# Row sums of the modulation traced in smaller portions, and eight weight casts moved from ACT to GpSimd, in a two-layer diffusion step

## The chip, the cores and the metric

The kernel runs on one core of a Trainium2 chip. The metric is the device time of one execution in microseconds. Times of a profile are counted from the start of its span.

## The reference

One inference step of a two-layer trunk over 128 context tokens and 512 latent tokens of 1024 features (640 tokens in five tiles of 128). Layer 0 is gated grouped-query attention, layer 1 a gated linear recurrence. Cut to what matters here:

```python
mod = silu(cond) @ ada_w[i] + ada_b[i]          # per layer: shift, scale, gate; cond is c (latent) or c_ctx (context)
sh, sc, g = split(mod, 3)
h = x * (1 + sc) + sh
# layer 0
q, k, v, gate = split(h @ w_in)                 # 16 query heads, 4 key heads of 64; gate of width 1024
q, k = rms_norm(q), rms_norm(k)                 # latent tokens also rotary
o = softmax(q k^T / 8) v                        # latent: over cache, context and latent keys
out = (o * silu(gate)) @ w_out
x = layer_norm(alpha * x + g * out)
# layer 1: the same around a gated recurrence (HGRN2, both directions)
```

## The kernel before

Matrix products run in a reduced-width 32-bit format and are kept accurate by splitting: each operand is a high part (a cast of the value) and a low part (the value minus its high part), and a product is three matmuls, high by high, high by low and low by high. Weights come from memory in pieces of 128 x 1024 into a ring of three raw buffers (`rawp`). `split_piece` (L232) takes the next raw piece, makes the high part on ACT (L240) and the low part on DVE or GpSimd (L241); `pump` issues the next loads on the SP queue in the fixed order of `order`.

The attention input weights are cut into chunks of 256 columns: 0 to 3 are queries (one chunk serves one key head), 6 to 9 the gate. The first half of the program, up to the end of attention, is traced in the order of the code and then ordered by a scheduler that plays a time line: on each engine it issues what is ready, and among ready instructions the one traced first. `keep_in_program_order` (`pin`) ties an instruction behind the one traced before it on its engine; all loads of this half on SP are tied so. `tc.issue_after(ins)` ties the instructions traced inside it to come after `ins`, if they are on the engine of `ins`. Buffers of a ring are handed out in traced order.

Stages of the first half:

- Lead-in, keys and values: the modulated input `hhi`/`hlo`, the key and value projection.
- `lead_in`, gate projection: query chunk 0 (`pmm`), then 16 half tiles (`gps`, L349 to L351, 24 matmuls each) of gate chunks 6 to 9, each ended by a SiLU on ACT (L854) into `gs`. The jobs in `later` (three query jobs `q_job`, four key splits) are taken one at every second step, and `settle` traces their transposes (`qps`, L702) one such step after. A query job on DVE is: scale by the norm (`qn`, L615), rotate (L654 to L658), cast the high part on ACT (L693), subtract on DVE (L694). The half tiles, the queries and the transposes share six PSUM places; three of them (`bank1`) hold the queries of chunk 0 until their jobs read them.
- Modulation of layer 1, shift and scale: 16 jobs (`COLS`), each a raw block of 128 x 1024 loaded on SP, and two row sums on DVE (`ada_cols`, L335: block times SiLU of the conditioning, summed along the row, for latent and context). Twelve jobs run in `lead_in` with blocks in a ring of two (`adar`, loads at L840); their product is spilled into the part of `gs` that is filled last. Four late jobs run in `cols_gen` within chunk 1 and take their blocks from the raw ring; they spill into the ring `s2` (two buffers, which the query and key splits use too).
- Attention over chunks 0 to 3 (`att_gen`), woven with a side stream: query chunks 1 to 3 (`q_gen`: weights, projection `qmm`, norm, split, transposes), each with a `fill` generator (chunk 1: the late jobs; chunks 2 and 3: the gate row of the modulation, `ada_gen`, matmuls at L284 with blocks `ada_s`), then `prefetch_gen`, which splits four pieces of the output weights (`wo_gen`), and the split of `gs`. A score tile (`sc`, L869 and L870) goes through a maximum on DVE (L964), an exponential on ACT (L969), a scaling on GpSimd (L975), transposes (L982), copies (L874) and the product with the values (L896). GpSimd also raises to the power -1/2 for the norms (L191).

The second half, the output projection and the recurrence, is issued in the order of the code.

Of the kernel before, what the change touches and what calls it, by code (L numbers as in the profile page):

```python
# [11 lines left out]
F32 = mybir.dt.float32  # L12
F32R = mybir.dt.float32r
U8 = mybir.dt.uint8
AF = mybir.ActivationFunctionType
ALU = mybir.AluOpType
AX = mybir.AxisListType

P = 128
D = 1024  # L20
KT = D // P
# [106 lines left out]
def drain(gen):  # L128
    for _ in gen:
        pass  # L130
# [3 lines left out]
def hybrid_step(ctx: ExitStack, tc: tile.TileContext, a: dict, o: dict):  # L134
    nc = tc.nc
    PSUM = bass.MemoryType.PSUM

    def pool(name, bufs, **kw):
        return tc.tile_pool(name=name, bufs=bufs, **kw)
# [15 lines left out]
    class Phase:  # L155
        def __init__(self, n2, n1):
            self.st = ExitStack()
            if n2:
                pools["b2"] = self.st.enter_context(pool("b2", n2, space=PSUM))
            pools.pop("b1", None)  # L160
            if n1:
                pools["b1"] = self.st.enter_context(pool("b1", n1, space=PSUM))
# [22 lines left out]
    shsc = [const.tile([P, 2, KT, 2], F32, name=f"shsc{i}") for i in range(2)]  # L185
# [43 lines left out]
            return a[name][c, i]  # L229
        return a[name][c][:, i * 1024:(i + 1) * 1024]  # L230

    def split_piece(hi, lo, src, lo_eng=None, after=()):  # L232
        pump()
        got, raw = ahead.popleft()
        assert got == src, (got, src)
        raw = raw[:, :hi.shape[-1]]
        with ExitStack() as st:
            for ins in after:
                st.enter_context(tc.issue_after(ins))
            nc.scalar.copy(hi, raw)  # L240
            (lo_eng or nc.gpsimd).tensor_tensor(lo, raw, hi.bitcast(F32), ALU.subtract)  # L241
        pump()

# [4 lines left out]
    def wtile(shape, dt, tag, name):  # L248
        ring = rings[turn[tag] % len(rings)]
        turn[tag] += 1  # L250
        return ring.tile(shape, dt, tag=tag, name=name)

    class Weights:


        def __init__(self, name, c, engs=None, after=()):
            self.h, self.l = [], []
            for i in range(2):
                hi = wtile([P, 1024], F32R, tag="whi", name="whi")
                lo = wtile([P, 1024], F32R, tag="wlo", name="wlo")  # L260
                split_piece(hi, lo, (name, c, i), engs and engs[i], after)
                self.h.append(hi[:].rearrange("p (k n) -> p k n", k=4))
                self.l.append(lo[:].rearrange("p (k n) -> p k n", k=4))

# [6 lines left out]
    def take(src):  # L271
        pump()
        got, raw = ahead.popleft()
        assert got == src, (got, src)
        return raw
# [52 lines left out]
            gate[0] = gsp.tile([P, 2, D], F32, tag="gate", name="gate0")  # L328
            gate_load(0, nc.gpsimd)

    def ada_cols(job, raw, spill):

        s, ft = job
        for c in range(2):
            nc.vector.scalar_tensor_tensor(spill, raw, 1.0, silb[:, c, :], ALU.mult, ALU.mult,  # L335
                                           accum_out=shsc[1][:, s, ft, c:c + 1])
        if ft == KT - 1:
            nc.vector.tensor_tensor(shsc[1][:, s], shsc[1][:, s], view(adab, (3 + s) * KT, [[1, KT], [0, 2]]), ALU.add)

    def cols_gen():  # L340
        for job in COLS[len(COLS) - COLS_LATE:]:
            ada_cols(job, take(("ada_c",) + job), prep.tile([P, D], F32, tag="s2", name="spill", bufs=2))
            pump()
            yield

    def feat_mms(ps, w, mt, j, hhi, hlo):
        c, t = slice(mt * P, (mt + 1) * P), slice(*HALVES[j])
# [5 lines left out]
    last_qmm = []  # L353
# [22 lines left out]
    PIECES = [(nh, i) for nh in range(2) for i in range(4)]  # L376
# [44 lines left out]
    silb = gsp.tile([P, 2, D], F32, tag="gate", name="silb")  # L421
# [7 lines left out]
    prep = pq.enter_context(pool("prep", 1))  # L429
# [155 lines left out]
    gs = gsp.tile([P, KT, NT], F32, tag="gs", name="gs")  # L585
# [101 lines left out]
    last_split = []  # L687
# [24 lines left out]

    def q_gen(c, X, fill):

        w = Weights("attn_w_in", c, (nc.vector, nc.vector), tuple(last_split))
        yield
        if c > 1:
            next(fill)
            yield
        pend = None  # L720
        for tt0, n in UNITS:
            ps = yield from tok_unit(w, tt0, n, "qmm")
            rstd = rms_stat(ps, n)
            r = rope_raw(ps, tt0, n, cosq, sinq, qg)
            yield
            if pend:
                for i in range(pend[1]):
                    pend[0](i)
                    yield
            next(fill, None)  # L730
            yield
            yield
            qn = rms_scale(r, n, rstd)
            yield
            pend = (q_split(qn, tt0, n, c % 2, X, bank1), n)
        yield
        for _ in fill:
            yield
        for i in range(pend[1]):
            pend[0](i)  # L740
            yield
# [11 lines left out]
    def lead_in(att):  # L753
# [59 lines left out]
        w = ws.pop(0)  # L813
        q0, kr = [], {}
        for n, (tt0, m) in enumerate(UNITS):
            ps = bank_any("pmm")
# [18 lines left out]
        raws = deque()  # L835

        def cols_load():
            if cols:
                raw = adar.tile([P, D], F32, tag="raw", name="adaraw")
                pin(nc.sync.dma_start(raw, piece(("ada_c",) + cols[0])))  # L840
                raws.append((cols.popleft(), raw))

        for _ in range(2):
            cols_load()
        step = 0
        for ch in range(6, 10):
            if ch < 9:
                ws[ch + 1] = Weights("attn_w_in", ch + 1, LEAD_LO)
            w = ws.pop(ch)
            for mt in range(2):  # L850
                for j, (t0, t1) in enumerate(HALVES):
                    ps = bank_any("gps")
                    feat_mms(ps, w, mt, j, hhi, hlo)
                    nc.scalar.activation(gs[:, 2 * (ch - 6) + mt, t0:t1], ps[:, :320], AF.Silu)  # L854
                    step += 1
                    if step % 2 or not later:
                        settle()
                    if step % 2 and later:
                        later.pop(0)()
                    if raws:  # L860
                        ada_cols(*raws.popleft(), gs[:, KT - 2:, :].rearrange("p a b -> p (a b)")[:, :D])
                        cols_load()
                    if step > 16 - EARLY:
                        next(att)
        assert not raws


    def score_mms(out, X, c, h, t0, k0, k1):
# [225 lines left out]

    wo = {}

    def wo_gen(layer, pieces, wpool):
        for nh, i in pieces:
            hi = wpool.tile([P, 1024], F32R, tag=f"wohi{nh}{i}", name="wohi")
            lo = wpool.tile([P, 1024], F32R, tag=f"wolo{nh}{i}", name="wolo")  # L1100
            wo[nh, i] = tuple(t[:].rearrange("p (k n) -> p k n", k=2) for t in (hi, lo))
            split_piece(hi, lo, ("attn_w_out" if layer == 0 else "rec_w_out", nh, i), nc.vector)
            yield

    def split_act(dst_hi, dst_lo, src, eng=None):
# [9 lines left out]
    woa = []  # L1115

    def prefetch_gen():
        wb.close()
        pq.close()
        woa.append(ws.enter_context(pool("woa", 1)))  # L1120
        yield from wo_gen(0, PIECES[:4], woa[0])

    def q_next(c):
        Xs[c] = xq[c % 2].tile([P, 4, NT], F32R, tag="X", name=f"X{c}")
# [651 lines left out]
```

## Time and profile before

| | |
|---|---|
| three runs | 846.48, 842.91, 846.51 us; median 846.48 |
| profiled execution | 844.78 us, span 843.0 us, granted TensorE clock 0.99 |
| TensorE (PE) busy | 808.0 us, 96% of the span |
| DVE busy | 559.9 us, 66% |
| ACT busy | 386.5 us, 46% |
| GpSimd (POOL) busy | 215.8 us, 26% |
| row sums in the lead-in | 24, the first at 71.6 us, the last at 122.0 us |
| row sums in chunk 1 | 8, from 144.3 to 185.5 us |

A row of the order of time gives the start, the length, the engine, the line, the operation, what it writes and reads, its size, and in brackets how long the engine was idle before it and for whom it waited. Rows of the same kind that follow each other are merged (x8). A row of the windows gives, for a stretch, its length, the busy time of PE, PEld, DVE, ACT and POOL with the number of instructions, the granted clock, the share of the DMA engines and GB/s. A row of the groups gives the count, the busy time, the mean in ns and the idle time of the engine before them with its causes.

### The profile page before, as it was taken

The page shows a single profiled execution, that of the slowest core. Times are in us where ns is not written, and L with a number is a line of the kernel's source. Part 1 is how long each engine was busy: PE and PEld are TensorE (multiplying, and loading weights), DVE is VectorE, ACT ScalarE, POOL GpSimd, SP SyncE. Part 2 cuts the span into 40 slices and gives each one's busy share as a digit, 9 for nine tenths or more (in the row PEclk, how much of TensorE's full clock was granted, in tenths as well). Part 3 has the DMA queues.
Part 4 walks back from the last instruction along what each step waited for, and adds up shares of the span by engine and source line. Part 5 has one row for each costly group of instructions (what it writes and reads, how often), then busy time and mean ns, then how long its engine had stood idle before and what let it go on. Part 6 is the DMA issues. An engine that isn't in the chain of part 4 may idle for free.

```text
span 843.0 us, 19206 instructions
## 1 busy us (share of the span) xinstructions
PE 808.0 (96%) x8025; PEld 729.2 (87%) x8025; DVE 559.9 (66%) x996; ACT 386.5 (46%) x782; POOL 215.8 (26%) x261
## 2 busy tenths in 40 slices
PE   8999899989999988999999999999999999999994
PEld 6789799878878766888999999999999999998774
DVE  4568882795657674776438575767668575858477
ACT  2252354674656776222434444435434544445232
POOL 0123001443344833010001304143333314121121
PEclk9999899999999999999999999999999999999998
DMA  9944451114151230630322322231322312324041
GB/s 325 397 145 165 151 175 52 51 54 148 51 200 51 101 100 1 225 125 35 108 69 68 103 72 82 83 109 51 107 89 83 99 61 89 120 65 157 23 161 75
DMA packets 34326, 93.28 MB, mean 111 GB/s; under 512 B 5040, under 2 KB 12224, under 8 KB 34240
## 3 DMA queue, kind: packets, MB, share of 16 engines
q1 hardware_dynamic: 23568, 74.10, 25.9%
q0 software_dynamic: 4768, 14.18, 5.4%
q10 hardware_dynamic: 5904, 3.78, 1.5%
q8 instruction: 63, 1.03, 0.5%
q14 instruction: 23, 0.19, 0.1%
HBM read 82.85 MB, written 9.19 MB: 109 GB/s over the span
## 4 chain that ended last, share of the span: by engine, by line
PE 82%; DVE 9%; ACT 2%; DMA 2%; issue 2%; POOL 1%; SPq 0%; DVEq 0%; ACTq 0%; POOLq 0%
PE rps L1319 7%; PE rps L1320 7%; PE rps L1321 7%; PE vgps L1309 5%; PE vgps L1311 5%; PE vgps L1310 5%; PE pot L896 4%; PE outp L1158 4%; PE outp L1160 3%; PE outp L1159 3%; PE pt L982 3%; PE lv L1452 2%; PE acc L536 2%; PE gps L349 2%; PE sc L869 2%
## 5 line engine op out<-in xcount | busy, mean ns | idle before, releaser
L1319 PE MATMUL rps<-h1hi,rhi 128*128 128x320 f32 x368 | 118.4, 322 | 0.0
L1320 PE MATMUL rps<-h1lo,rhi 128*128 128x320 f32 x368 | 113.9, 309 | 0.0
L1321 PE MATMUL rps<-h1hi,rlo 128*128 128x320 f32 x368 | 113.8, 309 | 0.0
L975 POOL TENSOR_SCALAR p<-p,rc 128x640 f32<-128x640 f32 x64 | 58.8, 921 | 116.6 <-DVE rc L974 102.3
L1319 PEld LDWEIGHTS rps<-h1hi,rhi 128*128 128x128 f32 x368 | 69.2, 188 | 1.3
L1320 PEld LDWEIGHTS rps<-h1lo,rhi 128*128 128x128 f32 x368 | 69.3, 188 | 0.0
L1321 PEld LDWEIGHTS rps<-h1hi,rlo 128*128 128x128 f32 x368 | 69.1, 188 | 0.0
L241 DVE TENSOR_TENSOR rlo<-raw,rhi 128x1024 fp32r<-128x1024 f32 x32 | 45.0, 1409 | 33.8 <-ACT rhi L240 33.8
L964 DVE TENSOR_REDUCE nm<-sc 128x1 f32<-128x640 f32 x64 | 52.0, 818 | 23.2 <-PE sc L870 22.8
L1480 POOL COPY At<-near 32x160 f32<-32x160 f32 x32 | 14.0, 438 | 196.8 <-DVE near L1442 195.8
L969 ACT ACTIVATE p<-sc,nm 128x640 f32<-128x640 f32 x64 | 51.2, 802 | 27.2 <-DVE nm L964 19.3
L240 ACT CAST rhi<-raw 128x1024 fp32r<-128x1024 f32 x32 | 33.6, 1049 | 52.0 <-PE rps L1320 48.8
L1430 ACT COPY kc<-A 128x640 f32<-128x640 f32 x40 | 32.2, 806 | 54.4 <-DVE A L1461 50.5
L1309 PE MATMUL vgps<-rhi,h1hi 128*128 128x256 f32 x180 | 51.5, 286 | 0.0
L1310 PE MATMUL vgps<-rlo,h1hi 128*128 128x256 f32 x180 | 50.9, 283 | 0.0
L1311 PE MATMUL vgps<-rhi,h1lo 128*128 128x256 f32 x180 | 50.9, 283 | 0.0
L982 PE MATMUL pt<-small,p 128*128 128x128 f32 x320 | 48.6, 276 | 1.4 <-ACT pts L874 0.9
L869 PE MATMUL sc<-kk,X 128*128 128x320 f32 x128 | 42.6, 343 | 6.1 <-ACT p L969 6.0
L874 ACT COPY pts<-pt 128x512 f32<-128x512 f32 x64 | 35.8, 591 | 24.4 <-PE pt L982 24.1
L982 PEld LDWEIGHTS pt<-small,p 128*128 128x128 f32 x320 | 37.1, 140 | 7.8 <-issue 5.3
L1309 PE MATMUL vgps<-wspare,h1hi 128*128 128x256 f32 x140 | 41.8, 298 | 0.0
L896 PE MATMUL pot<-pts,vv 128*64 128x256 f32 x320 | 38.9, 386 | 2.4 <-DVE pts L874 2.4
(301 smaller groups left out, 2423.6 us busy)
## 6 DMA issues: line engine op xcount, KB each, us to landing
raw<-in_rec_w_in SPq DMA_DIRECT2D x40, 512.0 KB, 3.7
raw<-in_ada_m SPq DMA_DIRECT2D x16, 512.0 KB, 8.0
raw<-in_attn_w_in SPq DMA_DIRECT2D x16, 512.0 KB, 4.2
raw<-in_ada_s SPq DMA_DIRECT2D x16, 512.0 KB, 4.4
adaraw<-in_ada_c SPq DMA_DIRECT2D x12, 512.0 KB, 3.8
raw<-in_attn_w_out SPq DMA_DIRECT2D x8, 512.0 KB, 4.1
raw<-in_rec_w_out SPq DMA_DIRECT2D x8, 512.0 KB, 3.5
x1d<-y SPq DMA_DIRECT2D x5, 512.0 KB, 2.6
```

The lines of the kernel that those rows point to most:

```text
L869: nc.tensor.matmul(out, X[:, h, t0:t0 + P], kk[:, c, k0:k1], start=True, stop=False)
L896: nc.tensor.matmul(pot[j * HD:(j + 1) * HD, :CW], vv[:, slot, c * HD:(c + 1) * HD], moving[j], start=first, stop=last)
L964: nc.vector.tensor_reduce(nm[:, 0:1], sc[:, :, :320], AX.XY, ALU.max, negate=True)
L969: return nc.scalar.activation(halves(p[:]), sc[:, :, :320], AF.Exp, bias=nm[:, 0:1], accum_out=su[:, 0:1])
L975: nc.gpsimd.tensor_scalar(p, p, rs[:, 0:1], 1.0, ALU.mult, ALU.mult)
L982: nc.tensor.transpose(pt[:, i * 256 + q * P:i * 256 + (q + 1) * P], ps[q][:, (k0 + i) * P:(k0 + i + 1) * P], ident)
L1309: nc.tensor.matmul(out, h1hi[:, k, t], hi, start=(k == 0), stop=False)
L1310: nc.tensor.matmul(out, h1hi[:, k, t], lo, start=False, stop=False)
L1311: nc.tensor.matmul(out, h1lo[:, k, t], hi, start=False, stop=(k == KT - 1))
L1319: nc.tensor.matmul(ps[:, j, :320], hi[:, k, :], h1hi[:, k, t], start=(k == 0), stop=False)
L1320: nc.tensor.matmul(ps[:, j, :320], hi[:, k, :], h1lo[:, k, t], start=False, stop=False)
L1321: nc.tensor.matmul(ps[:, j, :320], lo[:, k, :], h1hi[:, k, t], start=False, stop=(k == KT - 1))
```

## The change

- `ada_cols` becomes a generator: after each of its two row sums it yields, and each sum is traced inside `tc.issue_after` of an instruction that its caller names: the newest SiLU of the gate projection in `lead_in`, the newest query matmul in `cols_gen`.
- In `lead_in` a step advances this generator once in steps 1 to 6 and twice from step 7 on; before, each step ran one whole job. The next block is loaded when a job has ended, as before. Sums traced after the twelfth SiLU spill into the ring `s2`.
- In `cols_gen` each `next` of the fill now runs one sum, not a job.
- The high-part casts of query chunks 2 and 3 (four) and of the first four pieces of the attention output weights (four) are issued on GpSimd.

```diff
-    def split_piece(hi, lo, src, lo_eng=None, after=()):
+    def split_piece(hi, lo, src, lo_eng=None, after=(), hi_copy=None):
...
-            nc.scalar.copy(hi, raw)
+            (hi_copy or nc.scalar.copy)(hi, raw)
             (lo_eng or nc.gpsimd).tensor_tensor(lo, raw, hi.bitcast(F32), ALU.subtract)
...
-    def ada_cols(job, raw, spill):
+    def ada_cols(job, raw, spill, after):
 
         s, ft = job
         for c in range(2):
-            nc.vector.scalar_tensor_tensor(spill, raw, 1.0, silb[:, c, :], ALU.mult, ALU.mult,
-                                           accum_out=shsc[1][:, s, ft, c:c + 1])
+            with tc.issue_after(after()):
+                nc.vector.scalar_tensor_tensor(spill(), raw, 1.0, silb[:, c, :], ALU.mult, ALU.mult,
+                                               accum_out=shsc[1][:, s, ft, c:c + 1])
+            yield
...
+    def spare():
+        return prep.tile([P, D], F32, tag="s2", name="spill", bufs=2)
+
     def cols_gen():
         for job in COLS[len(COLS) - COLS_LATE:]:
-            ada_cols(job, take(("ada_c",) + job), prep.tile([P, D], F32, tag="s2", name="spill", bufs=2))
+            yield from ada_cols(job, take(("ada_c",) + job), spare, lambda: last_qmm[0])
             pump()
-            yield
...
-        w = Weights("attn_w_in", c, (nc.vector, nc.vector), tuple(last_split))
+        w = Weights("attn_w_in", c, (nc.vector, nc.vector), tuple(last_split),
+                    nc.gpsimd.tensor_copy if c > 1 else None)
...
+        silus = []
+
+        def spill():
+            return gs[:, KT - 2:, :].rearrange("p a b -> p (a b)")[:, :D] if len(silus) <= 12 else spare()
+
+        def cols_steps():
+            while raws:
+                yield from ada_cols(*raws.popleft(), spill, lambda: silus[-1])
+                cols_load()
+
+        cgen = cols_steps()
...
-                    nc.scalar.activation(gs[:, 2 * (ch - 6) + mt, t0:t1], ps[:, :320], AF.Silu)
+                    silus.append(nc.scalar.activation(gs[:, 2 * (ch - 6) + mt, t0:t1], ps[:, :320], AF.Silu).ins)
...
-                    if raws:
-                        ada_cols(*raws.popleft(), gs[:, KT - 2:, :].rearrange("p a b -> p (a b)")[:, :D])
-                        cols_load()
+                    for _ in range(1 if step < 7 else 2):
+                        next(cgen, None)
...
-    def wo_gen(layer, pieces, wpool):
+    def wo_gen(layer, pieces, wpool, hi_copy=None):
...
-            split_piece(hi, lo, ("attn_w_out" if layer == 0 else "rec_w_out", nh, i), nc.vector)
+            split_piece(hi, lo, ("attn_w_out" if layer == 0 else "rec_w_out", nh, i), nc.vector, (), hi_copy)
...
-        yield from wo_gen(0, PIECES[:4], woa[0])
+        yield from wo_gen(0, PIECES[:4], woa[0], nc.gpsimd.tensor_copy)
```

More of the change, by code (lines that the diff above doesn't have):

```diff
@@ L253, in hybrid_step, with __init__ @@
     class Weights:
-        def __init__(self, name, c, engs=None, after=()):
+        def __init__(self, name, c, engs=None, after=(), hi_copy=None):
             self.h, self.l = [], []
@@ L260, in __init__ @@
                 lo = wtile([P, 1024], F32R, tag="wlo", name="wlo")
-                split_piece(hi, lo, (name, c, i), engs and engs[i], after)
+                split_piece(hi, lo, (name, c, i), engs and engs[i], after, hi_copy)
                 self.h.append(hi[:].rearrange("p (k n) -> p k n", k=4))
@@ L859, in lead_in @@
                         later.pop(0)()
-                    if raws:
-                        ada_cols(*raws.popleft(), gs[:, KT - 2:, :].rearrange("p a b -> p (a b)")[:, :D])
-                        cols_load()
+                    for _ in range(1 if step < 7 else 2):
+                        next(cgen, None)
                     if step > 16 - EARLY:
                         next(att)
-        assert not raws
+        drain(cgen)
     def score_mms(out, X, c, h, t0, k0, k1):
```

## The prediction

> **What bounds the kernel now.** I read the page first, then the waits of TensorE, and then only the places where TensorE waits.
>
> ```profile
> PE 808.0 (96%) x8025; PEld 729.2 (87%) x8025; DVE 559.9 (66%) x996; ACT 386.5 (46%) x782; POOL 215.8 (26%) x261
> ```
>
> ```profile
> core 0 of [0], span 843.0 us
> engine line waited for: us in total, times, longest us
> PE sc L869 <- ACT p L969: 6.0, 10, 1.7
> PE qps L702 <- DVE qs L694: 4.9, 2, 3.9
> ```
>
> TensorE is busy 808.0 of 843.0 us, so an edit to other engines is worth only what it takes out of TensorE's waits, or adds to them. The change touches no matmul. Two rows of the waits fit it: one wait of 3.9 us for a query split on DVE, and score matmuls that wait for the exponentials of ACT. The order of time shows the first, in the gate projection:
>
> ```profile
> 86.09 0.31 PE L351 MATMUL gps<-hhi,wlo 128*128 128x320 f32 x1
> 90.33 1.23 PE L702 MATMUL qps<-identr,qs 128*128 128x128 f32 x8 [3.92 <-DVE qs L694]
> 91.78 0.64 PE L349 MATMUL gps<-hhi,whi 128*128 128x320 f32 x1 [0.22 <-ACT X L704]
> 92.21 0.47 PE L350 MATMUL gps<-hlo,whi 128*128 128x320 f32 x1
> ...
> 95.41 0.39 PE L350 MATMUL gps<-hlo,whi 128*128 128x320 f32 x1
> 95.64 0.31 PE L351 MATMUL gps<-hhi,wlo 128*128 128x320 f32 x1
> 95.78 0.31 PE L349 MATMUL gps<-hhi,whi 128*128 128x320 f32 x1
> ...
> 98.27 0.80 PE L702 MATMUL qps<-identr,qs 128*128 128x128 f32 x8
> ```
>
> ```profile
> 80.00:100.00 20.00, 15.85 (x99) 15.43 (x98) 18.48 (x32) 6.70 (x11) 2.41 (x1) 0.83 0.36 121
> 100.00:120.00 20.00, 20.00 (x144) 19.98 (x143) 16.13 (x27) 8.55 (x15) 0.00 (x0) 1.00 0.68 227
> 120.00:140.00 20.00, 20.00 (x150) 19.98 (x149) 5.50 (x9) 10.55 (x23) 0.00 (x0) 1.00 0.15 50
> ```
>
> TensorE stops at 86.40 (86.09 + 0.31). The next gate tile, at 91.78, waits for the bank that the cast X gives back, and that cast follows the transposes: with three of the single banks held by unfinished queries, TensorE has nothing else to start. After the stop it is slow: twelve steps from 92.21 to 95.41 take 3.20 us, 0.27 each, against 0.14 from 95.64 to 95.78, and the granted clock of that stretch is 0.83. So the stop costs 3.92 us of waiting, 0.22 for X, and some 2.2 us of low speed: 1.5 in the twelve steps (3.20 less 12 x 0.14), 0.3 in the step from 91.78 to 92.21, and 0.4 in the eight transposes (1.23, where a later set takes 0.80).
>
> What DVE did meanwhile:
>
> ```profile
> 71.59 1.22 DVE L335 SCALAR_TENSOR_TENSOR gs<-adaraw,silb 128x1024 f32<-128x1024 f32 x1
> ...
> 82.45 0.69 DVE L615 TENSOR_TENSOR qn<-pmm,rq 128x512 f32<-128x512 f32 x1 [0.85 <-POOL rq L191]
> 83.06 1.21 DVE L335 SCALAR_TENSOR_TENSOR gs<-adaraw,silb 128x1024 f32<-128x1024 f32 x1
> ...
> 85.40 1.22 DVE L335 SCALAR_TENSOR_TENSOR gs<-adaraw,silb 128x1024 f32<-128x1024 f32 x1
> ...
> 86.54 0.69 DVE L658 TENSOR_TENSOR r<-r,u 128x512 f32<-128x512 f32 x1
> 87.15 0.69 DVE L615 TENSOR_TENSOR qn<-pmm,rq 128x512 f32<-128x512 f32 x1
> 87.75 1.22 DVE L335 SCALAR_TENSOR_TENSOR gs<-adaraw,silb 128x1024 f32<-128x1024 f32 x1
> ...
> 89.49 0.69 DVE L694 TENSOR_TENSOR qs<-r,qs 128x512 fp32r<-128x512 f32 x1
> ```
>
> Counted from the first at 71.59, the sixth, seventh and eighth row sums (L335) stand between the normalised query and its split, and the last two delay the split by 1.14 us each (85.40 to 86.54; 87.75 to 88.89, where the next instruction starts). The scheduler of this half puts an instruction that is ready into any hole of a dependent chain, and a hole of tenths then costs 1.14.
>
> **The row sums, part by part.** Their number stays: 24 here, 8 in chunk 1. The new order call does not hold them: it ties only what is traced on the engine of the instruction it is given, and that is an ACT activation (a matmul in chunk 1), while the sums run on DVE. What does change is the order of tracing: one sum a step for six steps, then two; and a raw block is loaded when its job ends, so the load's place on SP moves.
>
> ```profile
> 62.64 11.67 SPq L219 DMA_DIRECT2D raw<-in_attn_w_in  x2
> 76.05 13.28 SPq L840 DMA_DIRECT2D adaraw<-in_ada_c  x4
> 89.38 8.68 SPq L219 DMA_DIRECT2D raw<-in_attn_w_in  x2
> 98.10 10.95 SPq L840 DMA_DIRECT2D adaraw<-in_ada_c  x4
> ...
> 186.72 34.00 SPq L219 DMA_DIRECT2D raw<-in_ada_s  x8
> ```
>
> SP issues in traced order. Before, four modulation loads (76.05) go ahead of the weights of chunk 9 (89.38). After, one does, at step 3; the next is traced at step 5, behind both weight loads, and the second of these is not issued before about 97.7 (89.38 + 8.68, less its own 0.3), when a raw buffer comes free. So only three jobs, six sums, have their data before that. The seventh and eighth (85.40 and 87.75) go from the chain, 2 x 1.14 = 2.28 us. The sixth (83.06) stays. The wait falls from 3.92 to about 1.65 us. That so short a stop leaves the clock alone has a row:
>
> ```profile
> 299.75 1.04 ACT L240 CAST wohi<-raw 128x1024 fp32r<-128x1024 f32 x1 [0.28 <-DMA raw<-in_attn_w_out]
> 300.70 0.79 ACT L969 ACTIVATE p<-sc,nm 128x640 f32<-128x640 f32 x1
> ```
>
> ```profile
> 301.63 0.41 PE L869 MATMUL sc<-kk,X 128*128 128x320 f32 x1 [1.71 <-ACT p L969]
> ```
>
> ```profile
> 300.00:320.00 20.00, 17.61 (x135) 13.06 (x136) 11.68 (x27) 13.67 (x34) 9.16 (x11) 1.00 0.22 71
> ```
>
> TensorE waited 1.71 us here and the clock of the stretch stayed at 1.00. Stops between 1.71 and 3.92 us are not in the trace; I take it that 1.65 is on the safe side. The gain is 2.28 + 2.2 = 4.4 us (the 0.22 for X stays). Its ends: 2.3 if the clock falls all the same; 6.3 if the stop goes whole; nothing if the scheduler fills the two holes with other work of DVE.
>
> The six sums that leave 83 to 97 us come back later in the lead-in, some 7 us of DVE. I cost them at nothing: DVE is busy 16.13 and 5.50 of 20 us in the two stretches from 100 to 140, so 18 us are free there, while TensorE runs through without a stop. The last of them use the split ring's buffers (two, shared with the key splits) and end close to the first score maxima; if that cover is short, one sum of 1.14 us stands ahead of it.
>
> **The late sums of chunk 1.** Before, a fill step held both sums of a job; after, it holds one, so three sums lie in the three units and five in the drain behind the third. A job's raw block is free only after its second sum, and the raw ring (three buffers) feeds the next weights and then the gate blocks:
>
> ```profile
> 182.68 1.40 DVE L335 SCALAR_TENSOR_TENSOR spill<-raw,silb 128x1024 f32<-128x1024 f32 x1
> ...
> 185.48 1.21 DVE L335 SCALAR_TENSOR_TENSOR spill<-raw,silb 128x1024 f32<-128x1024 f32 x1
> ...
> 190.11 0.64 PE L284 MATMUL adaps<-raw,sil 128*32 128x256 f32 x8 [1.15 <-DMA raw<-in_ada_s]
> ```
>
> The last sum ends near 186.7, SP issues the first gate block at 186.72, and TensorE waits 1.15 us for it. With five sums behind the third unit where two stood, this load goes out three sums, 3.4 us, later, and the weights of chunk 2 with it. If TensorE keeps its order, that is 3.4 us more, and 2.2 of low speed if the clock falls: 5.6. If the scheduler, which knows of the buffers, gives TensorE transposes and scores in the meantime, it is nothing; a gain is possible, since three sums leave a busy DVE earlier in chunk 1, up to one sum of 1.14. I take +1.0, near the free end, as attention has probabilities ready ahead.
>
> **The eight casts.** ACT loses 8 x 1.04 us (row at 299.75), GpSimd takes them.
>
> ```profile
> L975 POOL TENSOR_SCALAR p<-p,rc 128x640 f32<-128x640 f32 x64 | 58.8, 921 | 116.6 <-DVE rc L974 102.3 <-PE adaps L284 5.0 <-DVE shsc L338 3.6
> ...
> L1107 POOL TENSOR_TENSOR hlo<-gs,hhi 128x640 fp32r<-128x640 f32 x6 | 9.3, 1557 | 0.8 <-ACT hhi L1106 0.8
> ```
>
> The trace has no such cast on GpSimd. By elements, one input costs 0.921 x 1.6 = 1.47 us, two inputs 1.557 x 1.6 = 2.49. A cast reads one, so I take 1.5: 0.4 more than on ACT, ahead of a low part on DVE that follows. What is gained on ACT is seen at 299.75: the cast stood 0.28 us for its block and ran 1.04, the exponential (300.70) came behind it, and TensorE waited 1.71 for that. Gone: 1.3 us. The other seven I cost at nothing, cover being weights that are split ahead of their use. Ends: -2.6 if a second of the four output casts held an exponential as long; +3.2 if each of the eight makes DVE wait 0.4 and TensorE with it. Two things wait behind a cast on GpSimd: the scaling of probabilities and the power of the query norm. The casts of chunks 2 and 3 also lose their hold behind the last split, which named an ACT and a DVE instruction; they may start earlier.
>
> One row speaks against putting them there:
>
> ```profile
> 289.17 2.52 DVE L694 TENSOR_TENSOR qs<-qn,qs 128x256 fp32r<-128x256 f32 x1
> ...
> 289.85 1.55 POOL L1107 TENSOR_TENSOR hlo<-gs,hhi 128x640 fp32r<-128x640 f32 x1
> ```
>
> A split of 256 columns, half of that at 89.49 (0.69), takes 2.52 us beside GpSimd work, and ends (291.69) when that ends (291.40).
>
> The Trainium skill's page SBUF — State Buffer (the section on the engine side of the ports) says why: GpSimd and a DVE operation with two SBUF inputs lock one port pair, held for the whole instruction, and the loser fully blocks. The trace agrees at 289.17. By that rule each cast can block the low-part subtraction of another piece, or a row sum, for its full 1.5 us; it is the third rival below.
>
> **The sum.** -4.4 - 1.3 + 1.0 = -4.7 us. The profiled execution took 844.78 us (843.0 of span and 1.8 around it), between the three runs' lowest of 842.91 and median of 846.48. From 844.78: 840.1 us. About 0.5% (4.2 us) is what a measurement can tell from no change here; the forecast is just past it.
>
> **Rivals.**
> First, the change does not hold the sums, and the order on SP doesn't help: other DVE work goes into the holes, or the scheduler moves the transposes forward as the chain gets shorter, so that TensorE meets the same wait earlier. For it: the order call ties nothing on DVE. Against: the loads must pass SP. The lead-in stays as it is; with the rest (-0.3) that is 844.5.
> Second, slower: the late sums. TensorE starves between 187 and 194 for the gate block and the chunk 2 weights: +5.6 instead of +1.0, and the lead-in gives only 2.3, because its clock falls too: 844.8 - 2.3 - 1.3 + 5.6 = 846.8; should the lead-in give nothing, 849.1. It decides once the stop near 190 exceeds some 3 us. For it: the chain of 182 to 190 is tight already (a wait of 1.15). Against: score and transpose work is there.
> Third, the port lock: half of the eight casts block DVE on the path for 1.5 us: +6.0, no gain on ACT, late sums +1.0: 844.8 - 4.4 + 6.0 + 1.0 = 847.4. For it: the row at 289.17; against: GpSimd is busy 26%.
> Fourth, all goes: the stop in the lead-in vanishes (-6.3), ACT's casts give 2.6 and the late sums cost nothing: 835.9.
>
> **How the numbers follow.** Forecast 0.45, in its own range 838 to 842.5: 0.29 of it past 0.5%, 0.16 within. First rival 0.20: within 0.15, slower 0.05, as a new order may cost. Second 0.13, third 0.10: slower 0.20, within 0.03. Fourth 0.12: faster. So faster 0.41, same 0.34, slower 0.25. The range from 835 to 848 takes in the fourth, the first, the third and the near end of the second; some 2 in 10 stay out.
>
> **What would show it.** Right: fewer than nine L335 before the first split of queries, the one weight load of chunk 9 on SP ahead of the fourth modulation load, a stop at the first qps under 2 us with a clock of 1.00 from 80 to 100; no cast L240 on ACT between exponentials near 300. Wrong: the stop of 3.9 us still there; a stop over 3 us at L284; DVE rows of low parts well over 1.2 us beside casts on GpSimd of more than 2.5 us.

## The result and the profile after

The changed kernel takes 853.26 us (median of six runs), the kernel before 845.13 us beside it: ratio 1.0097, 95% interval 1.007 to 1.0123, some 8 us slower. Forecast were 840.1 us and a range up to 848. The profiled execution took 854.26 us, span 852.5.

The page of the changed kernel, and its waits of TensorE (total, times, longest):

```profile
PE 815.1 (96%) x8025; PEld 732.6 (86%) x8025; DVE 563.5 (66%) x996; ACT 379.2 (44%) x774; POOL 228.6 (27%) x269
```

```profile
PE sc L884 <- ACT p L984: 9.5, 14, 3.0
PE qps L706 <- DVE qs L698: 3.0, 2, 1.9
...
PE adaps L284 <- DMA raw<-in_ada_s: 1.8, 1, 1.8
```

The wait for the query split fell from 4.9 to 3.0 us, but scores now wait 9.5 us for exponentials where it was 6.0, and TensorE's busy time grew by 7.1 us with the same 8025 matmuls: it ran slower. The windows (length; PE, PEld, DVE, ACT and POOL busy; granted clock; DMA share; GB/s) show where; first the row of before that was not shown yet, then the kernel after:

```profile
180.00:200.00 20.00, 17.33 (x147) 14.65 (x146) 12.81 (x33) 11.57 (x24) 6.82 (x8) 1.00 0.39 136
```

```profile
80.00:100.00 20.00, 17.76 (x117) 17.38 (x116) 12.87 (x20) 7.73 (x14) 1.90 (x1) 0.91 0.23 75
180.00:200.00 20.00, 14.08 (x89) 10.36 (x90) 15.76 (x31) 5.68 (x13) 10.72 (x8) 0.74 0.46 159
300.00:320.00 20.00, 16.05 (x89) 11.61 (x89) 14.70 (x25) 10.67 (x24) 11.82 (x13) 0.83 0.22 79
```

The lead-in's clock rose from 0.83 to 0.91, but two stretches that ran at 1.00 fell to 0.74 and 0.83. The clock was at half for 10.2 us from 188.5 on, and for 6.8 us from 307.9 on. The order of time around the first of them, by engine (TensorE, DVE, ACT, GpSimd, SP):

```profile
186.22 0.41 PE L884 MATMUL sc<-kk,X 128*128 128x320 f32 x1 [1.09 <-ACT p L984]
...
190.08 0.63 PE L884 MATMUL sc<-kk,X 128*128 128x320 f32 x1 [3.01 <-ACT p L984]
...
193.34 1.08 PE L284 MATMUL adaps<-raw,sil 128*32 128x256 f32 x8 [1.83 <-DMA raw<-in_ada_s]
```

```profile
185.09 1.21 DVE L336 SCALAR_TENSOR_TENSOR spill<-raw,silb 128x1024 f32<-128x1024 f32 x1
...
186.23 2.05 DVE L336 SCALAR_TENSOR_TENSOR spill<-raw,silb 128x1024 f32<-128x1024 f32 x1
...
188.21 0.81 DVE L979 TENSOR_REDUCE nm<-sc 128x1 f32<-128x640 f32 x1
...
189.01 1.20 DVE L336 SCALAR_TENSOR_TENSOR spill<-raw,silb 128x1024 f32<-128x1024 f32 x1
```

```profile
189.14 0.80 ACT L984 ACTIVATE p<-sc,nm 128x640 f32<-128x640 f32 x1 [2.97 <-DVE rc L989]
```

```profile
185.43 1.77 POOL L240 CAST whi<-raw 128x1024 fp32r<-128x1024 f32 x1 [0.80 <-DMA raw<-in_attn_w_in]
```

```profile
190.25 9.19 SPq L219 DMA_DIRECT2D raw<-in_ada_s  x5
```

Two late row sums stand ahead of a score maximum (188.21, L979); the exponential behind it comes at 189.14, and TensorE stops for 3.01 us. The last sum ends at 190.2, SP issues the gate block at 190.25, and TensorE stops again for 1.83 us.

From here on, three stages of TensorE are compared in each trace: the **lead-in** (start of the first `gps` matmul to start of the sixth half tile; before 72.17 to 97.10), the **border** (end of the last high-by-high query matmul, `qmm` of L358 in the kernel before, of chunk 1 to that of chunk 2; 177.78 to 226.07), and **near 300** (end of the last such matmul of chunk 3 to the last `pot` matmul; 279.02 to 336.29). After against before: -2.45, +7.55 and +3.78 us. With the start (-0.39), the rest of the way to the border (+0.22), chunk 3 (+0.08) and all that follows (+0.67) that is the 9.46 us by which the spans differ.

### The profile page after: what moved, and what is told of

Same layout as the page of the kernel before. It is cut to its first block, busy times and chain, and to the rows that moved or that the text cites. A ratio compares the mean times of both kernels' runs of the same rounds, so it can differ in the third digit from the quotient of the medians.

```text
span 852.5 us, 19209 instructions
## 1 busy us (share of the span) xinstructions
PE 815.1 (96%) x8025; PEld 732.6 (86%) x8025; DVE 563.5 (66%) x996; ACT 379.2 (44%) x774; POOL 228.6 (27%) x269
## 3 DMA queue, kind: packets, MB, share of 16 engines
q10 hardware_dynamic: 5904, 3.78, 1.4%
q8 instruction: 63, 1.03, 0.5%
## 4 chain that ended last, share of the span: by engine, by line
PE 84%; DVE 9%; issue 2%; ACT 2%; DMA 2%; POOL 1%; SPq 0%; DVEq 0%; ACTq 0%; POOLq 0%
PE rps L1334 7%; PE rps L1335 7%; PE rps L1336 7%; PE vgps L1324 5%; PE pot L911 4%; PE vgps L1325 4%; PE vgps L1326 4%; PE outp L1173 4%; PE pt L997 3%; PE outp L1175 3%; PE outp L1174 3%; PE acc L540 3%; PE lv L1467 2%; PE sc L884 2%; PE gps L353 2%
## 5 line engine op out<-in xcount | busy, mean ns | idle before, releaser
L990 POOL TENSOR_SCALAR p<-p,rc 128x640 f32<-128x640 f32 x64 | 63.3, 991 | 113.0 <-DVE rc L989 108.4
L979 DVE TENSOR_REDUCE nm<-sc 128x1 f32<-128x640 f32 x64 | 51.9, 816 | 13.3 <-PE sc L885 12.8
```

The source lines that it names most:

```text
L979: nc.vector.tensor_reduce(nm[:, 0:1], sc[:, :, :320], AX.XY, ALU.max, negate=True)
L990: nc.gpsimd.tensor_scalar(p, p, rs[:, 0:1], 1.0, ALU.mult, ALU.mult)
```

## The experiments

Theory: the lead-in gains; the late sums lose at the border. Rival: the casts on GpSimd do the harm, by holding DVE. The order call is out of both: it ties an instruction only behind one on its own engine, and the ones that it names here are on ACT and TensorE, while the sums run on DVE.

All the kernels are in this table: ratio to the kernel before with its interval, and the three stages of one profiled execution against before, in us. The stages leave out chance differences at the program's start, so they are the finer measure; but each is of one execution and holds its half clock (kernels 1 and 13 have the same lead-in, the second with 3.4 us at half clock: -3.98 and -2.65).

```
                                   ratio (95% interval)     lead-in border near 300
changed kernel                     1.0097 (1.0070, 1.0123)  -2.45   +7.55   +3.78
1  lead-in sums                    0.9953 (0.9930, 0.9975)  -3.98   -0.08    0.00
2  late sums                       1.0103 (1.0072, 1.0135)  -0.20   +6.81   +1.73
3  query casts                     1.0060 (1.0038, 1.0082)  +0.08   +4.92   -0.48
4  output casts                    0.9972 (0.9953, 0.9991)  +0.30    0.00   -2.17
5  all but late sums               1.0057 (1.0034, 1.0080)  -2.53   +2.48   +1.80
6  1 and 4                         0.9943 (0.9923, 0.9963)  -3.98   -0.07   -2.21
7  3, low parts behind last sum    1.0075 (1.0047, 1.0104)  -0.39   +5.17   -0.51
8  6 with three late jobs          0.9917 (0.9886, 0.9948)  -2.13   -1.95   -2.19
9  3, casts behind the power       1.0009 (0.9991, 1.0028)  +0.44   +1.28   -0.56
10 5 with 9; fourth cast on ACT    1.0048 (1.0028, 1.0067)  -3.98   +1.18   +5.63
11 late sums as 3, 3, 2            0.9989 (0.9971, 1.0007)  +0.51   -1.96   -0.10
12 8, sums held behind the split   0.9903 (0.9869, 0.9936)  -5.08   -1.96   -2.17
13 10, fourth cast behind, GpSimd  1.0007 (0.9985, 1.0030)  -2.65   +1.16   +1.68
14 12 with the casts of 13         0.9952 (0.9935, 0.9970)  -5.08   +0.13   +0.99
15 12 with chunk 2's casts of 9    0.9912 (0.9880, 0.9944)  -5.08   +0.15   -2.06
16 12 with chunk 3's casts of 9    0.9896 (0.9854, 0.9939)  -5.08   -1.96   +0.04
```

**Each part alone (1 to 4).** Against the kernel before:

```diff
 kernel 1, lead_in:   -ada_cols(*raws.popleft(), ...)        # both sums of a job in a step
                      +for _ in range(1 if step < 7 else 2):
                      +    next(cgen, None)
 kernel 2, cols_gen:  -ada_cols(job, take(...), ...); pump(); yield
                      +yield from ada_cols(job, take(...), ...); pump()
 kernel 3, q_gen:     +nc.gpsimd.tensor_copy if c > 1 else None
 kernel 4, wo_gen:    +woa[0], nc.gpsimd.tensor_copy
```

> Only the lead-in half of the change: one row sum a step, then two, with the modulation loads' new place on SP; late sums and casts as before. Theory (the lead-in gains, but less than forecast): the stop at the first transposes falls from 3.92 to 1.85 us, TensorE's low clock after it lasts some 3.4 us instead of 6.8, and the gate projection ends 2.8 us earlier; -2.8 us at the end, since nothing else moves. Rival (the lead-in only moves time): the 2.8 us are given back by attention's start or in chunk 1, and the end moves by less than 1 us.

> Only the late half: one row sum for each fill of chunk 1, five in the drain behind the third unit; lead-in and casts as before. Theory (late sums starve TensorE): score maxima come behind the sums, the gate blocks and the weights of chunk 2 load some 3.5 us later, TensorE waits 3 us for an exponential and 1 to 2 us for the gate block near 190, and its clock falls for 7 to 10 us: +5 to +7 us between the end of chunk 1's queries and the start of chunk 2's. Rival (the casts on GpSimd do it, by holding DVE beside them): without them the five sums run at 1.2 us each, and the end moves by +1 us or less.

> Only the four high-part casts of query chunks 2 and 3 go to GpSimd; sums and the output weights' casts as before. Theory (late sums starve TensorE): the casts cost 1.0 to 1.8 us each on GpSimd but lie ahead of their use, and the end moves by -1 to +1 us. Rival (casts hold DVE): two-input operations of DVE beside them take some 2 us for 1.2, the chunk 2 weights are ready 2 us later, TensorE's clock falls near 190, and the end is 4 to 7 us later.

> Only the first four high-part casts of the output weights go to GpSimd. Theory (queue): the casts wait behind the scaling of probabilities on GpSimd, the low parts on DVE come some 8 us later and stand ahead of score maxima, TensorE waits 1 us for an exponential near 307 and its clock falls: +3 to +4 us, against the 1.3 us forecast as a gain. Rival (it is a follow-up of the late start): with chunk 1 undisturbed the exponential at 300 no longer stands behind a cast on ACT and the end is 1 us earlier.

The lead-in gave 4.0 us, all of it kept, where I had forecast 2.8 with 3.4 us of low clock. In its trace the stop is that of the changed kernel, but the clock stayed up:

```profile
86.37 0.85 PE L708 MATMUL qps<-identr,qs 128*128 128x128 f32 x8 [1.85 <-DVE qs L700]
```

```profile
80.00:100.00 20.00, 17.76 (x128) 17.37 (x128) 14.06 (x21) 8.28 (x16) 0.42 (x1) 1.00 0.23 80
```

The late sums alone cost 8.7 us, with all casts on ACT, and most of it at the border: the rival that the casts make this loss falls. Theirs is the same pair of stops, and the same two sums ahead of a score maximum:

```profile
187.64 0.61 PE L886 MATMUL sc<-kk,X 128*128 128x320 f32 x1 [2.14 <-ACT p L986]
...
193.23 1.08 PE L284 MATMUL adaps<-raw,sil 128*32 128x256 f32 x8 [2.02 <-DMA raw<-in_ada_s]
```

```profile
185.45 1.39 DVE L336 SCALAR_TENSOR_TENSOR spill<-raw,silb 128x1024 f32<-128x1024 f32 x1
...
186.77 1.21 DVE L336 SCALAR_TENSOR_TENSOR spill<-raw,silb 128x1024 f32<-128x1024 f32 x1
...
187.91 0.81 DVE L981 TENSOR_REDUCE nm<-sc 128x1 f32<-128x640 f32 x1
```

TensorE's idle time at the border is 5.94 us there (3.17 before); the rest of the 6.81 us went with 10.2 us at half clock. The 1.73 us near 300 went with half clock alone: 6.8 us of it, while TensorE idles less than before (5.59 us for 6.54).

The query casts lose too (+5.1), against the theory, and the output casts gain (-2.4), against it as well.

**What the query casts do (5 to 7, 9).** Kernel 5 is the changed kernel without the edit of 2; 6 is the edits of 1 and 4.

```diff
 kernel 7:  Weights(..., tuple(last_split + last_sum), nc.gpsimd.tensor_copy ...)
 kernel 9:  Weights(..., tuple(last_split + last_pow), nc.gpsimd.tensor_copy ...)
```

`last_sum` is the newest row sum (DVE), so the low parts go behind it; `last_pow` is the newest power of the query norm (GpSimd), so the casts go behind it.

> The change without its late sums (both sums of a job in one fill, as before); lead-in and the eight casts as in the change. Theory (the late sums are the largest loss, and the query casts make a loss of their own at the same place): -4.0 from the lead-in, -2.4 from the output weights' casts, +5 from the query casts, as alone: -1.5 us against before, and TensorE's wait at the gate block near 185 is still 3 us. Rival (the query casts lose only together with late work): the wait near 185 is 1 us as before and the end is 6 us earlier than before.

> The lead-in sums and the output weights' four casts alone. Theory: neither touches the stretch from 175 to 200, so both gains stand and add: -4.0 - 2.4 = -6.4 us. Rival (the casts' gain of 2.4 us was a shift of order by chance): with everything 6 us earlier the order near 300 falls otherwise and the end is at -4 us.

> The query casts on GpSimd as in the run with them alone, and the low parts of chunks 2 and 3 on DVE queued behind the last row sum: on DVE one row sum and the pair of low parts change places, some four rows move on TensorE, nothing else. Theory (the loss is that the last row sum, and with it the raw block for the first gate weights, comes behind the two low parts): the gate weights load 2.9 us earlier, TensorE's wait for them falls from 3.3 to about 1 us, the clock stays up near 190, and 4 of the 5 us are back. Rival (the casts themselves hold DVE and TensorE): the end stays 4 to 5 us behind before.

> The four query casts on GpSimd, each queued behind the power of the query norm of the unit before it, so that no cast that waits for its block stands ahead of that power. Theory (head of the queue: in the run with the casts alone the second cast stood 3.0 us for its block, and the power behind it made the last query split, the last row sum, the low parts and the gate weights' load some 2.5 us late): the power is back at 180, the wait for the gate weights falls from 3.3 to about 1.2 us, the clock near 190 stays up, and the end is within 1 us of before. Rival (GpSimd holds DVE's two-input operations, or the casts there are too slow): the end stays 3 to 5 us behind before, with DVE rows of 2 us beside the casts.

Kernel 7 missed: the low parts and the last sum changed places and the border stayed at +5.2. The first gate block goes out when the first of them is done (187.97 in kernel 3, behind a low part; 190.01 in kernel 7, behind the sum), so their order is not the cause. The cause stands earlier, on GpSimd; kernel 3:

```profile
180.93 1.04 POOL L240 CAST whi<-raw 128x1024 fp32r<-128x1024 f32 x1 [3.00 <-DMA raw<-in_attn_w_in]
181.93 1.02 POOL L191 TENSOR_TENSOR rstd<-rs_t,mhalf 128x4 f32<-128x4 f32 x1
```

```profile
191.13 1.08 PE L284 MATMUL adaps<-raw,sil 128*32 128x256 f32 x8 [3.31 <-DMA raw<-in_ada_s]
```

```profile
179.39 0.15 DVE L190 TENSOR_SCALAR rs_t<-ss 128x4 f32<-128x4 f32 x1
```

The second cast stood 3.00 us for its block, and the power behind it, whose input was ready at 179.5 (the row of L190), waited with it. The query split, the sum, the low parts and the gate block follow from that power. Kernel 9 puts the casts behind it:

```profile
180.16 1.02 POOL L191 TENSOR_TENSOR rstd<-rs_t,mhalf 128x4 f32<-128x4 f32 x1 [2.04 <-DVE rs_t L190]
181.14 2.22 POOL L241 CAST whi<-raw 128x1024 fp32r<-128x1024 f32 x2
```

```profile
190.62 0.64 PE L285 MATMUL adaps<-raw,sil 128*32 128x256 f32 x8 [0.53 <-DMA raw<-in_ada_s]
```

The wait for the gate block falls from 3.31 to 0.53, the clock of 180 to 200 is 1.00 (0.83 in kernel 3), and the kernel is level with before (1.28 of the 4.92 us remain at the border). So the loss was the head of the queue, and the half clock behind it: kernel 5, whose wait for the gate block was as long (3.42 us) but whose clock stayed up, loses 2.48 us at the border where kernel 3, with 6.8 us at half clock, loses 4.92. An in-order queue whose first instruction waits for a transfer holds all behind it. The Trainium skill's page TensorE: Matmul & The Clock Gate (section on the array of 16 tiles) states that ACT, DVE and GpSimd take their queues strictly in order; the trace agrees, 3.00 us here. Kernel 5 missed its forecast of -1.5 us (+4.8): the output casts' gain had turned into a loss near 300 (below). Kernel 6 came to -4.8 for -6.4 forecast; its stages are those of 1 and 4 added.

**How many sums stand behind the third unit (8, 11).**

```diff
 kernel 8, on 6:             -COLS_LATE = 4
                             +COLS_LATE = 3
 kernel 11, on before, in cols_gen:
                             +for _ in ada_cols(job, take(...), ...):
                             +    n += 1
                             +    if n % 3 == 0: yield
```

> As the lead-in sums with the output weights' casts, but only three modulation jobs are left for chunk 1 (one for each of its three units, none in the drain) and 26 sums lie in the lead-in. Theory (what starves TensorE near 185 is the row sums behind the third unit): the gate weights load 2 us earlier, the wait of 1.1 us for them goes, and the end is 1 us earlier than that kernel, -7.4 us against before. Rival (the two sums that are added at the end of the lead-in stand ahead of the first score maxima): TensorE stops 1 to 2 us near 136 and the end is at -5 us or later.

> The kernel before with the eight row sums of chunk 1 as three, three and two for its units, none behind the third; casts and lead-in as before. Theory (what counts is how many sums lie behind the third unit: five cost 8.7 us, two were there before): the gate weights load 2 us earlier, TensorE's wait for them (1.15 us) goes, -1 to -2 us. Rival (the eight sums cost by their number on DVE, and the kernel with three late jobs was faster because it had six): within 0.5 us of before, with the wait at another place of chunk 1.

Kernel 8 came to -7.0 us for -7.4 forecast. With none behind the third unit the border gives 1.95 and 1.96 us, whether six sums or eight lie in chunk 1; with two (before) 0, with five +6.81. So it is the place, not the number. The ratio of kernel 11 alone would not settle it. In kernel 8 the gate matmuls have no wait:

```profile
183.96 0.64 PE L284 MATMUL adaps<-raw,sil 128*32 128x256 f32 x8
```

**The sums really held (12).**

```diff
-                yield from ada_cols(*raws.popleft(), spill, lambda: silus[-1])
+                yield from ada_cols(*raws.popleft(), spill, lambda: last_split[1] if step > 5 else silus[-1])
```

> As the lead-in sums with three late jobs and the output weights' casts on GpSimd, but from the sixth step on the lead-in's sums are tied to the split of the queries on DVE, so that they are really held: the sixth sum leaves the chain too. Theory (each row sum in a hole of the chain costs its 1.14 us, and a shorter stop leaves the clock alone): the stop at the first transposes falls from 2.2 to about 1.0 us, no low clock near 90, -1.1 us against that kernel, -8 against before. Rival (the chain has another hole that other DVE work fills): the stop stays at 2 us.

`last_split[1]` is the subtraction on DVE, so here the call ties. The sixth sum leaves the chain, and the stop, 1.85 us in kernel 1, falls by 1.10, about one sum. In kernel 8, on which this one is an edit, it was 2.17 us with 3.4 us of half clock behind it, so the lead-in goes from -2.13 to -5.08:

```profile
86.75 0.84 PE L708 MATMUL qps<-identr,qs 128*128 128x128 f32 x8 [0.75 <-DVE qs L700]
```

The kernel takes 836.68 us beside 844.61, -8.2 us for -8 forecast: it beats both, with no query cast on GpSimd.

**Near 300 (10, 13 to 16).**

```diff
 kernel 10, on 5 with the tie of 9, in wo_gen:
      -split_piece(..., nc.vector, (), hi_copy)
      +split_piece(..., nc.vector, (), hi_copy if i < 3 else None)
 kernel 13, the same place:
      +if hi_copy and i == 3:
      +    for _ in range(12):
      +        yield
      +split_piece(..., nc.vector, tuple(last_scale) if hi_copy and i == 3 else (), hi_copy)
 kernel 14: the edits of 12 and the ties of 13
 kernels 15, 16, on 12 with the tie of 9:
      +nc.gpsimd.tensor_copy if c == 2 else None      # 16: c == 3
```

`last_scale` is the newest scaling (GpSimd); the twelve empty steps put it some scalings after the third cast.

> The change without its late sums, the query casts queued behind the power as in the run above, and the fourth output cast back on ACT, since it was the one that stood 5 us at the head of GpSimd's queue. Theory: both heads of the queue gone, the lead-in's 4.0 us and the output casts' 2 us come out: -5 to -6 us against before, where the change without late sums gave +4.8. Rival (more work on GpSimd delays the scalings anyway): +2 us or more remain.

> As the run with the query casts behind the power and the fourth output cast on ACT, but all four output casts on GpSimd and the fourth queued behind a scaling that lies nine scalings after the third cast. Theory (whichever engine has the fourth cast at the head of its queue while its block is loaded makes TensorE wait: 5.3 us stood on GpSimd, 3.75 us on ACT): the cast waits under 1 us, TensorE's stop of 3.1 us near 302 and the low clock after it go, and the end is 5 to 6 us earlier than before. Rival (with the query casts on GpSimd the low parts of the output weights come late on DVE, and that alone holds the score maxima): the stretch from 290 to 310 keeps 3 us or more of stops and the end is at -2 us or later.

> All four parts in the form that the runs so far speak for: lead-in sums held behind the query splits, three late jobs with none behind the third unit, query casts behind the power, the fourth output cast behind a later scaling. Theory (each part loses only through what stands behind it in a queue): -8 to -10 us against before, as fast as the kernel without the query casts or faster. Rival (the query casts on GpSimd cost even when placed): 2 us or more slower than the kernel that holds the sums and has no query casts on GpSimd (-8.2 us).

> The fastest kernel so far (lead-in sums held, three late jobs, output casts on GpSimd) with the two query casts of chunk 2 on GpSimd, behind the power; those of chunk 3 stay on ACT. The order on GpSimd near 300 stays that of the fastest kernel: the fourth output cast behind the last split of the gates. Theory (what loses near 300 is an order that only chunk 3's casts bring about): the stretch from 270 to 330 takes as long as without query casts, and the end is at -6 to -8 us against before. Rival (any query cast on GpSimd costs the 4.5 us): -4 us.

> The same with the two query casts of chunk 3 on GpSimd and those of chunk 2 on ACT. The fourth output cast lies ahead of the last split of the gates on GpSimd, as in the change. Theory: the fourth cast stands 5 us for its block, the scalings behind it are late, the stretch from 270 to 330 is 5 to 8 us longer, and the end is between -3 us and no gain. Rival (any query cast costs the 4.5 us in its own chunk): the loss is between 225 and 245, and the stretch from 270 on is as without query casts.

In kernel 5, as in the changed kernel, the fourth output cast stood 5 us for its block, with the scalings behind it; in kernel 6 the scheduler had put it after another split:

```profile
306.94 1.64 POOL L240 CAST wohi<-raw 128x1024 fp32r<-128x1024 f32 x1 [5.31 <-DMA raw<-in_attn_w_out]
```

```profile
301.88 1.54 POOL L240 CAST wohi<-raw 128x1024 fp32r<-128x1024 f32 x1 [0.43 <-DMA raw<-in_attn_w_out]
```

On ACT (kernel 10) it stood 3.75 us and held an exponential:

```profile
305.20 0.41 PE L887 MATMUL sc<-kk,X 128*128 128x320 f32 x1 [3.14 <-ACT p L987]
```

The forecast of kernel 10, -5 to -6 us, missed (+4.1). Placed behind (13), that stop is 1.03 us and the loss near 300 falls from 5.63 to 1.68; the 6.8 us at half clock that kernel 10 has in this stage go with it. But the output casts' gain of 2.2 does not come back, and my forecast of -5 to -6 us missed (+0.6). Kernel 14, all parts placed, was forecast at -8 to -10 us and came to -4.1. Kernel 16 shows that the wait is not the whole cause:

```profile
296.34 1.69 POOL L241 CAST wohi<-raw 128x1024 fp32r<-128x1024 f32 x1 [5.25 <-DMA raw<-in_attn_w_out]
```

There the cast stands 5.25 us and the stage loses nothing against before, it only fails to gain; I had forecast 5 to 8 us more in this stretch.

What kernels 5, 10, 13, 14, 16 and the changed one share is chunk 3's query casts together with the output casts: in all six TensorE has the same three stops of 0.46, 0.7 and 1.1 us there; with chunk 2's alone (15) the gain of 2.06 us is back, as I had forecast. The three stops mark another order, but they are not its price: they add up to 2.3 us, and kernels 12 and 15 have two of 0.9 and 1.34 us in their place. Kernel 16 is 2.2 us longer than kernel 12 in this stage with 0.4 us more idle time of TensorE, and with eight more matmuls (four for scores, four transposes), which in kernel 12 lie in chunk 3; chunk 3 is no shorter for it (52.46 us beside 52.51). So chunk 3's casts bring about an order near 300 that costs 2 us or more in this stage; why the scheduler arrives at it, I did not settle.

In the changed kernel TensorE idles no longer there than before (6.02 us for 6.54): its 3.78 us go with those eight matmuls and with 6.8 us at half clock. Chunk 2's casts, even behind the power, cost 2.1 us at the border (15 against 12), where kernel 15 has a stop of 1.35 us for an exponential that kernel 12 has not. Kernels 12, 15 and 16 can't be told apart by their ratios.

## Why the prediction was wrong, step by step

- **The order call ties nothing, and SP's order moves the loads: right.** Six sums lie before the first split and the next at 100.11, as forecast.
- **The lead-in, -4.4 us: right in kind.** Alone it measured -4.0 (stage -3.98): 2.07 of waiting (2.28 forecast; 1.85 us of stop remain for 1.65) and 1.91 of low clock. In the changed kernel it was -2.45, since the clock fell for 3.4 us. The step "I take it that 1.65 is on the safe side" failed: one row of a stop that leaves the clock alone is no rule. Among the traces, the stop of 1.85 us left the clock alone in kernels 1, 6 and 10 and not in 13 and the changed one (the last section says what goes with it). That kernel 1 gained 4.0 us of the 4.4 forecast is in part luck: half clock took 1.5 us of it in the changed kernel.
- **The lead-in's sums at no cost: right.** The last ended at 135.13, ahead of the first maximum, with no stop there.
- **The late sums, +1.0: the main failure.** Alone they cost 8.7 us. The step was "near the free end, as attention has probabilities ready ahead": attention did not, since the same sums stood ahead of its score maxima on DVE (2.14 and 3.01 us of stops for exponentials). So the far end, 5.6, was too low as well: it held the gate block's delay and 2.2 us of low clock, not a stop for the exponentials, and not 10.2 us at half clock.
- **The eight casts, -1.3.** The output casts alone gave -2.4, the end that I had named for a second exponential held. "The other seven I cost at nothing, cover being weights that are split ahead of their use" failed: the query casts cost 5.1 us (4.92 at the border, with 6.8 us at half clock). I had written what waits behind a cast on GpSimd, and that these casts may start earlier, and had priced only the cast's length, not its wait at the head of the queue. The length was the harmless part: 1.03 us measured, for 1.5 taken.
- **The rivals.** The second came nearest, with its place (near 190) and its lead-in (2.3 us given, 2.45 measured), at 853 for the 846.8 to 849.1 given: it kept the casts' gain and had one stop. The stop over 3 us that it named was for an exponential (3.01); the gate block, for which it let TensorE starve, gave 1.83. The third, the port lock, is in the rows: a row sum took 2.05 us and the cast beside it 1.77, where the same sum without casts (kernel 2, at 186.77) took 1.21. The 0.84 us more stand ahead of the maximum at 188.21, and about as much is the stop longer than in kernel 2 (3.01 for 2.14). But it is the small part: kernel 2 has no cast there and loses 6.81 of the 7.55 us, and kernel 9, where a cast takes 1.23 us and the DVE product beside it 1.25 (0.50 in the changed kernel), is level with before. The Trainium skill's rule that was weighed there (SBUF — State Buffer) holds, and was not the main cause. The sum was also wrong in kind: it added parts that were priced apart, and at the border the late sums and the query casts delay the same gate block (+6.81 and +4.92 alone, +7.55 in the changed kernel), while near 300 the output casts' gain turns into a loss beside the query casts.

## What to carry to other kernels

Before moving an instruction to another in-order queue, price not its length but the wait that it may stand in front, and look for what is queued behind it. Work that "only" moves within an engine is free if no bound stage begins behind it: here row sums cost nothing in the lead-in, lost 8.7 us when five lay behind the third unit, and gave 2 us at the border when none was left there. Small edits that meet in one stretch do not add: test them there together and apart.

## What was not expected of the hardware

- The granted clock falls on a fixed grid. In each trace with more than one fall they begin whole multiples of 3.413 us apart (before: at 10.24, 88.74 and 836.26 us, the later two 23 and 242 steps after the first) and last 3.4, 6.8 or 10.2 us; the last fall of each trace runs past its end. The Trainium skill's page TensorE: Matmul & The Clock Gate (section on what is happening) gives a free-running window of 3.4 us, with which that agrees; its advice to avoid gaps over some 3 us (section on why this matters for kernels) is no safe bound here, as 1.85 us was enough.
- A fall goes less by the length of a stop than by how much of one step of this grid TensorE is busy. From 60 to 825 us, the 18 traces hold 18 steps at full clock in which a matmul ran for less than 41% of the time, and the clock fell behind each of them. It fell behind 5 of the 18 steps with 45 to 59%, and behind none of the 3946 busier ones. So the stop of 1.85 us left 36% of its step busy in the changed kernel, where the clock fell, and 67% in kernel 1, where the grid split the stop and the clock stayed up. In between it is open: at 46% the clock fell in kernel 13 and not in kernel 10. At the border kernel 3's stop of 3.31 us left 33% in one step, and the clock fell; kernel 5's 3.42 us were split and left 52 and 47%, and it stayed up. Where the grid lies changes from one execution to the next.
- A 128 x 1024 cast took 1.03 us on GpSimd, no more than the 1.04 on ACT; only beside a two-input operation of DVE did it take up to 1.77.
